# A second filling rate for the end of the RWKV stage in a hybrid recurrent layer

## The chip, the cores and the metric

The kernel runs on one core of a Trainium2 chip. The time is device microseconds (us) of one launch; before the change the median of three runs is 1621.25 us (1619.7 to 1624.62). The change is measured against that. One execution was taken with the hardware profiler; the rows below come from it, with times in us from the start of its span.

## What is computed

One layer of a bidirectional diffusion backbone on 640 tokens (512 latent, 128 context), width 1024, in float32. Three mixers share one projection of the normalised input; gates merge them; a SwiGLU feed-forward follows:

```python
(hq, hf_f, hf_b, hi, hg, rw, mq, mk, mv, mo, mg, gates) = _split(h @ P['w_in'][l], IN_WIDTHS)
y_a, new_a = _hgrn2(hq, hf_f, hf_b, hi, hg, ...)      # gated linear recurrence, 4 heads
y_b, new_b = _rwkv7(rw, grid, ...)                    # RWKV-7: delta-rule scan, 8 heads
y_c, new_c = _mlstm(mq, mk, mv, mo, mg, ...)          # matrix memory, 4 heads
g_a, g_b, g_c = jnp.split(jax.nn.sigmoid(gates.astype(F32)), 3, axis=-1)
merged = g_a * (y_a @ wb[0]) + g_b * (y_b @ wb[1]) + g_c * (y_c @ wb[2])
x = x + g1 * _rms(merged @ P['w_out'][l], nw[1])
u, gt = jnp.split(h @ P['w_ffn_in'][l], 2, axis=-1)
x = x + g2 * _rms((silu(gt) * u) @ P['w_ffn_out'][l], nw[3])
```

The scale, shift and gate vectors `sh1 .. g2` are `silu(cond) @ w_ada` in six pieces; the last four of them are needed only after the merge.

## The kernel before

Activations lie transposed, channels on partitions, tokens along the free dimension in two halves of 320 (`HN`). A float32 product is made of three passes over split operands (`whi`, `wlo` for weights; `h_hi`, `h_lo` for activations). One block of 128 output channels is a **projection**: one 512 KB weight load on the DMA queue of SyncE (SP), two casts `whi` on ScalarE (ACT), two subtractions `wlo` on VectorE (DVE), and 2 halves x 8 blocks x 3 passes = 48 matmuls of 128x320 into two PSUM tiles `pj`. GpSimd (POOL) has no part in it.

The stages follow each other: the input norm with a first part of the conditioning; RWKV; HGRN and mLSTM woven together (called the mixer stage here); merge and output projection; feed-forward.

RWKV goes over four pairs of heads (`p`), and in each pair over three groups of chunks (`gi`). A group has a wide part, `prepare(gi)` (the inverse of a triangular matrix by doubling: products `q`, `y2`, `xp`, `rr`, `dy`), and a chain of dependent steps, `scan(gi)`: per chunk three small products into one tile `z` (from the state `Ss`, from `zs`, from `SV`), with VectorE and ScalarE between any two, and at the end the output products `oc`. `weave` runs `scan(gi - 1)` beside `prepare(gi)`. After the last group nothing of RWKV is left to run beside `scan(2)`; `finish` then normalises the output (`rwkv_post`, head sums `hs`).

Work that nothing in RWKV waits for is used as **filling**. The generator `fill()` holds, in the order of the string `ORDER`, 24 gate projections (`g`), 4 + 4 projections for HGRN and mLSTM output gates (`h`, `o`), each evacuated by ScalarE into a tile `gs` and stored to DRAM (`gates`), and 16 conditioning units (`a`: two 512 KB loads `wada`, 8 row products `acc`, a ScalarE copy `rows`, and two products `col_` that the next unit issues). A projection takes two pulls of the generator, of which the first issues all its work; a conditioning unit takes one. The tail of the order is `gga` repeated, 5 pulls each.

`run_over` decides when a pull is made. It adds `rate[at[0]]` for every step of the main work and pulls one item for every whole unit:

```python
def run_over(main, under, rate):
    a = 0.0
    for _ in main:
        a += rate[at[0]]
        while a >= 1.0:
            a -= 1.0
            next(under, None)
```

`at[0]` is the number of the pair, and `FILL` has one rate for each pair. In the mixer stage the same function runs with `FILL2`, one rate for each mLSTM head; what is left of the filling after that stage is issued by `run(fl)` behind it. The instructions of all this go to a scheduler that places them on the five engines' queues, each in order; the steps of RWKV have a priority ahead of the filling (`OFFD`). So the tables `FILL` and `FILL2` decide near which step of the main work a projection stands, and the scheduler decides between which of its instructions.

In the mixer stage an HGRN head has per level two operand tiles `hT` (made by GpSimd, VectorE and ScalarE) and a product `hg_`; a level ends in `hAT` or `hAD`, and after the last level come the output products `hop`, transposes `hotr`, and the result `ya`. The mLSTM head beside it has products `ms`, `kv`, `kx`, `np_`, `nq`. The first products of the merge are `pj<-ya,whi`.

The mLSTM part begins with its gates: a projection `mg`, evacuated to `G`, then a chain over ScalarE and VectorE (`LF`, the scans `gc` and `mrow`, `PK`). ScalarE's queue holds the evacuation of HGRN's first projection (`hT<-pj`, line 396) and the exponential `PK` (line 1308) in one order; TensorE's transposes `btr` (line 557) wait for the first.

Of the kernel before, what the change touches and what calls it, by code (L numbers as in the profile page):

```python
# [36 lines left out]
SPO = ()  # L37
PADD = (1, 3, 5, 7)
FRONT = 0.25
FILL = (0.145, 0.145, 0.16, 0.155)  # L40
WRES = 10
ADAB = 12
RB2 = 2
# [212 lines left out]
def build(tc, **A):  # L256
# [36 lines left out]
    with ExitStack() as top:  # L293
# [246 lines left out]
        def weave(*streams):  # L540

            live = [[g, r, 0.0] for g, r in streams]
            while live:
                x = min(live, key=lambda a: a[2])
                try:
                    next(x[0])
                    x[2] += 1.0 / x[1]
                    yield
                except StopIteration:
                    live.remove(x)  # L550
# [56 lines left out]
        at = [0]  # L607

        def first(g, offset):

            while True:
                try:
                    if offset:
                        with tc.high_priority(offset):
                            next(g)
                    else:
                        next(g)
                except StopIteration:
                    return
                yield  # L620
# [9 lines that stand above are left out]
# [5 lines left out]
        with ExitStack() as rs:  # L635
# [377 lines left out]
            def front_ahead():  # L1013

                for x in fr:
                    yield
                    while at[0] < 3 and Rs[at[0] + 1].get("ready"):
                        yield

            def chain(*gens):  # L1020
                for g in gens:
                    yield from g

            def finish(p):
                rwkv_post(p, Rs[p]["osum"], Rs[p]["wg"], Rs[p]["yb"])
                yield

            def rwkv():
                last = None
                for p in range(4):  # L1030
                    while not Rs[p].get("ready"):
                        yield next(fr)
                    at[0] = p
                    elem, prepare, scan = rwkv_pair(p, Rs[p])
                    for gi in range(3):
                        g = chain(elem(), prepare(0)) if gi == 0 else prepare(gi)
                        yield from weave((last, SRATE[p]), (g, 1.0)) if last else g
                        last = scan(gi)
                        if gi == 2:
                            last = chain(last, finish(p))  # L1040
                yield from last

            run_over(weave((first(rwkv(), OFFD), 1.0), (first(front_ahead(), OFFF), FRONT)), fl, FILL)

        with ExitStack() as ms, ExitStack() as mr:
# [786 lines left out]
```

## Time and profile before

| | |
|---|---|
| median of 3 runs | 1621.25 us (1619.7 to 1624.62) |
| the profiled execution's own time | 1623.08 us |
| its span, first to last instruction | 1621.3 us |
| mean granted TensorE clock | 0.976 of 2.4 GHz |
| busy TensorE / VectorE / ScalarE / GpSimd | 95% / 70% / 48% / 17% |
| RWKV's last group alone, to the end of its outputs | 562.76 to 589.25 us |
| last mixer head, first `htr` to first merge product | 957.49 to 1003.03 us |

The profiled execution is 1.83 us above the median of the runs, and 1.78 us of its time lie around the span. A matmul's duration in a row includes its pipeline, so matmuls in a row start every 0.147 us and show 0.31 us each; distances between starts are the time they take. A granted clock of 1.00 is 2.4 GHz and 0.50 is 1.2 GHz.

### The profile page before, as it was taken

To read this page: it belongs to the slowest core of one execution; us is meant where nothing else is said; L and a number is where in the kernel's file an instruction comes from. 1 tells how busy PE (TensorE), PEld (TensorE's weight loads), DVE (VectorE), ACT (ScalarE), POOL (GpSimd) and SP (SyncE) were. 2 spreads that over 40 slices of the span, in tenths; PEclk is the share of its full clock that TensorE was granted. 3 is DMA by queue.
4 is the path that set the end of the run, shared out by engine and by line. 5 is a ranking of instruction groups with operands and counts; after the bars stand their busy time and mean duration, and the time that the engine had idled before them with its cause. 6 is when DMAs were issued, how large, how long until landed. Compare 5 with 4: busy or idle time off the path is not lost. (4 is left out here: it accounts for less than half of the span.)

```text
span 1621.3 us, 34724 instructions
## 1 busy us (share of the span) xinstructions
PE 1540.6 (95%) x14194; PEld 1418.1 (87%) x14194; DVE 1131.9 (70%) x2355; ACT 782.8 (48%) x1546; POOL 275.7 (17%) x347
## 2 busy tenths in 40 slices
PE   6999999999999988899999999999999999999996
PEld 2988888888877778889798988999999999999996
DVE  6788788687777644786758578772887386586576
ACT  5364455454454334666476666223553343243244
POOL 2110110110110100211303031000123241341211
PEclk9999999999999969999999999999989999999998
DMA  9222222212122313232332332643512222222322
GB/s 361 71 75 88 74 71 80 95 50 88 66 73 95 113 49 103 70 99 78 94 100 85 100 101 95 201 145 108 155 37 86 95 79 76 82 88 68 99 94 97
DMA packets 63791, 157.35 MB, mean 97 GB/s; under 512 B 7432, under 2 KB 27912, under 8 KB 63504
## 3 DMA queue, kind: packets, MB, share of 16 engines
q1 hardware_dynamic: 63488, 155.13, 29.5%
q8 instruction: 111, 1.82, 0.5%
q14 instruction: 48, 0.39, 0.1%
q10 hardware_dynamic: 144, 0.00, 0.0%
HBM read 136.73 MB, written 18.37 MB: 96 GB/s over the span
## 5 line engine op out<-in xcount | busy, mean ns | idle before, releaser
L277 PE MATMUL pj<-h_hi,whi 128*128 128x320 f32 x1560 | 495.0, 320 | 5.4 <-ACT t L396 2.7
L277 PE MATMUL pj<-h_lo,whi 128*128 128x320 f32 x1560 | 494.4, 317 | 0.0
L277 PE MATMUL pj<-h_hi,wlo 128*128 128x320 f32 x1560 | 493.2, 317 | 0.0
L262 DVE TENSOR_TENSOR wlo<-raw,whi 128x512 fp32r<-128x512 f32 (+1 forms) x318 | 228.5, 726 | 130.7 <-ACT whi L344 106.2
L277 PEld LDWEIGHTS pj<-h_hi,whi 128*128 128x128 f32 x1560 | 296.3, 191 | 12.0 <-ACT t L396 3.7
L277 PEld LDWEIGHTS pj<-h_lo,whi 128*128 128x128 f32 x1560 | 296.7, 190 | 3.2
L277 PEld LDWEIGHTS pj<-h_hi,wlo 128*128 128x128 f32 x1560 | 296.9, 190 | 2.8
L344 ACT CAST whi<-raw 128x512 fp32r<-128x512 f32 (+1 forms) x264 | 156.8, 599 | 219.6 <-PE pj L277 209.4
L277 PE MATMUL pj<-a,whi 128*128 128x320 f32 x704 | 155.3, 309 | 0.0
L277 PEld LDWEIGHTS pj<-a,whi 128*128 128x128 f32 x704 | 117.7, 188 | 0.2
L277 PE MATMUL pj<-a,wlo 128*128 128x320 f32 x352 | 108.8, 309 | 0.0
L277 PE MATMUL pj<-t_hi,whi 128*128 128x320 f32 x288 | 89.1, 309 | 1.1 <-DVE u L262 1.1
L277 PE MATMUL pj<-t_hi,wlo 128*128 128x320 f32 x288 | 89.1, 309 | 0.1
L277 PE MATMUL pj<-t_lo,whi 128*128 128x320 f32 x288 | 89.0, 309 | 0.0
L262 DVE TENSOR_TENSOR wlo<-sm,whi 128x512 fp32r<-128x512 f32 x72 | 68.1, 946 | 11.4 <-ACT whi L1684 8.5
L1684 ACT CAST whi<-sm 128x512 fp32r<-128x512 f32 x72 | 44.4, 621 | 64.4 <-PE pj L277 50.2
L1678 POOL TENSOR_TENSOR sm<-raw 128x512 f32<-128x512 f32 x36 | 49.0, 1360 | 110.3 <-DMA raw<-wff 72.5
L277 PEld LDWEIGHTS pj<-a,wlo 128*128 128x128 f32 x352 | 66.1, 188 | 0.0
L277 PE MATMUL pj<-hl,whi 128*128 128x320 f32 x256 | 56.5, 310 | 0.6 <-ACT hl L1462 0.6
L1684 ACT CAST whi<-raw 128x512 fp32r<-128x512 f32 x54 | 33.5, 620 | 45.6 <-PE pj L277 37.7
L277 PEld LDWEIGHTS pj<-t_hi,whi 128*128 128x128 f32 x288 | 54.1, 188 | 1.3 <-DVE u L262 1.3
L277 PE MATMUL acc<-raw,sc 128*32 128x256 f32 (+1 forms) x320 | 40.7, 437 | 14.8 <-DMA raw<-wada 14.8
(659 smaller groups left out, 2988.0 us busy)
## 6 DMA issues: line engine op xcount, KB each, us to landing
raw<-wmix SPq DMA_DIRECT2D x76, 512.0 KB, 3.5
raw<-wada SPq DMA_DIRECT2D x48, 512.0 KB, 5.6
raw<-wff SPq DMA_DIRECT2D x44, 512.0 KB, 3.7
gates<-gs SPq DMA_DIRECT2D x64, 160.0 KB, 1.8
raw<-wff SPq DMA_DIRECT2D x24, 384.0 KB, 3.2
gs<-gates SPq DMA_DIRECT2D x24, 320.0 KB, 3.1
raw<-wbr SPq DMA_DIRECT2D x12, 512.0 KB, 4.3
raw<-wout SPq DMA_DIRECT2D x8, 512.0 KB, 5.0
```

Of the source, the lines that this page charges most:

```text
L262: dve.tensor_tensor(out, a, b, op)
L277: newest[0] = pe.matmul(out, lhsT=lhsT, rhs=rhs, start=start, stop=stop, skip_group_check=more).ins
L344: act.copy(hi[:, :w], raw[:, o:o + w])
L1678: pool.tensor_tensor(o, x, y, op)
L1684: act.copy(hi, x)
```

## The change

The rate table gets a fifth entry, and when the last group of the last pair begins, `at[0]` is set to 4, which selects it. The rate of that group goes from 0.155 to 0.34; the steps before it keep 0.155. `front_ahead`, which also reads `at[0]`, is exhausted by then. Nothing else differs.

```diff
-FILL = (0.145, 0.145, 0.16, 0.155)
+FILL = (0.145, 0.145, 0.16, 0.155, 0.34)
...
                     for gi in range(3):
+                        if p == 3 and gi == 2:
+
+                            at[0] = 4
                         g = chain(elem(), prepare(0)) if gi == 0 else prepare(gi)
```

From there to the end of RWKV the main work has 28 steps (19 of `prepare(2)`, 5 of `scan(1)`, 4 of `scan(2)` with `finish`). With the remainder carried in, 0.155 makes 5 pulls of them (two projections and a conditioning unit) and 0.34 makes 10 (four and two). Five pulls are exactly one period `gga`, so every later pull finds the same kind of item at the same step as before, one period on. In the mixer stage 21 pulls are made either way. Before, five pulls were left for `run(fl)` after that stage (one projection, one conditioning unit and the last columns among them); now none is left, and the mixer stage's last pull issues the last columns where it issued a projection.

How the queues move, at three places. **TensorE, the last scan of RWKV** (`z`, from the last product `dy` of `prepare(2)` on). Before:

```order
L277 MATMUL z<-Ss,AX_7763 64x64 x2
L277 MATMUL z<-Ss,AX_7792 64x64 x2
L277 MATMUL z<-zs,Yf 64x64 x4
L277 MATMUL z<-SV,BT_7784 64x64 x2
L277 MATMUL z<-SV,BT_7834 64x64 x2
L277 MATMUL z<-Ss,AX_7763 64x64 x2
L277 MATMUL z<-Ss,AX_7792 64x64 x2
L277 MATMUL z<-zs,Yf 64x64 x4
```

Now:

```order
L277 MATMUL z<-Ss,AX_7763 64x64 x2
L277 MATMUL z<-Ss,AX_7792 64x64 x2
L277 MATMUL pj<-h_lo,whi 128x320
L277 MATMUL pj<-h_hi,wlo 128x320
L277 MATMUL pj<-h_hi,whi 128x320
L277 MATMUL pj<-h_lo,whi 128x320
L277 MATMUL z<-zs,Yf 64x64 x4
L277 MATMUL pj<-h_hi,wlo 128x320
L277 MATMUL pj<-h_hi,whi 128x320
L277 MATMUL pj<-h_lo,whi 128x320
L277 MATMUL pj<-h_hi,wlo 128x320
L277 MATMUL pj<-h_hi,whi 128x320
```

Where steps of the scan stood next to each other, runs of 4 to 5 projection matmuls stand between them. The same holds back to the end of `scan(1)`: from the `z<-zs` at 562.76 us to the end of `oc`, 76 of the 96 moved matmuls stand in 16 runs of 3 to 7; two stand just ahead of it, and 18, with the 8 row products of the conditioning unit, between `oc` and the projection `mg`.

**TensorE, the last mixer head** (last levels `hg_`, ahead of the output products `hop`). Before:

```order
L277 MATMUL kv<-vs,mkt 128x129
L277 MATMUL pj<-h_hi,wlo 128x320
L277 MATMUL pj<-h_hi,whi 128x320
L277 MATMUL pj<-h_lo,whi 128x320
L277 MATMUL hg__12926<-hq,hT_12924 32x32 x20
L277 MATMUL pj<-h_hi,wlo 128x320
L277 MATMUL np__13000<-v_8302,mD 128x129
L277 MATMUL kv<-vs,mkt 128x129
L277 MATMUL np__13000<-v_8302,mD 128x129 x2
L277 MATMUL pj<-h_hi,whi 128x320
```

Now:

```order
L277 MATMUL hg__12897<-hT_12887,hT_12886 32x32 x20
L277 MATMUL hg__12930<-hT_12920,hT_12919 32x32 x20
L277 MATMUL kx<-vs,mkt 128x129
L277 MATMUL hg__12970<-hT_12960,hT_12959 32x32 x20
L277 MATMUL hg__13022<-hT_13012,hT_13011 32x32 x20
L277 MATMUL kv<-vs,mkt 128x129
L277 MATMUL hg__13077<-hq,hT_13075 32x32 x20
L277 MATMUL np__13151<-v_8453,mD 128x129 x2
L277 MATMUL kv<-vs,mkt 128x129
L277 MATMUL np__13151<-v_8453,mD 128x129
```

Four levels follow each other with no projection between them; from the first `htr` of this head on, none is left.

**ScalarE, the beginning of the last mixer head** (`hkt` copies the transposes `htr`; `gs` evacuates the projection that stands just ahead of them on TensorE). Before:

```order
L572 ACTIVATE gs<-pj 128x320
L344 CAST whi<-raw 128x512 x2
L1138 COPY hkt<-htr 128x512
L572 ACTIVATE gs<-pj 128x320
L558 COPY mkt<-btr 128x384
```

Now:

```order
L572 ACTIVATE gs<-pj 128x320
L344 CAST whi<-raw 128x512 x2
L1465 CAST hl<-yc 128x640
L572 ACTIVATE gs<-pj 128x320
L1141 COPY hkt<-htr 128x512
L558 COPY mkt<-btr 128x384
```

The second `gs` stands ahead of `hkt` instead of behind it, and a cast `hl` of the merge stage has come in (two more stand a few rows on).

## Rows read from the trace of the kernel before

**Rows 1.** The page: busy time of two engines, and the granted clock in 40 slices.

```profile
PE 1540.6 (95%) x14194; PEld 1418.1 (87%) x14194; DVE 1131.9 (70%) x2355; ACT 782.8 (48%) x1546; POOL 275.7 (17%) x347
...
PEclk9999999999999969999999999999989999999998
```

**Rows 2.** Stretches of the span: length, then busy us (and instructions) of TensorE's matmuls and weight loads, VectorE, ScalarE and GpSimd, the granted clock, the DMA engines' share and GB/s. The first two are RWKV's end, the other four the last mixer head.

```profile
562.76:589.25 26.49, 18.38 (x283) 14.56 (x282) 9.87 (x30) 4.38 (x13) 3.24 (x8) 0.57 0.17 66
589.25:600.85 11.60, 10.91 (x59) 10.29 (x59) 3.25 (x8) 7.10 (x12) 1.43 (x3) 0.81 0.29 87
957.49:968.77 11.28, 9.42 (x89) 7.25 (x86) 6.81 (x17) 5.67 (x13) 4.64 (x6) 1.00 0.56 138
968.77:973.30 4.53, 3.81 (x99) 3.33 (x98) 1.46 (x4) 1.53 (x6) 3.25 (x3) 1.00 0.63 242
973.30:992.86 19.56, 17.68 (x300) 15.94 (x300) 18.82 (x49) 10.05 (x20) 4.52 (x7) 1.00 0.18 52
992.86:1003.03 10.17, 9.17 (x79) 7.81 (x78) 8.15 (x31) 8.15 (x26) 0.00 (x0) 1.00 0.20 68
```

**Rows 3.** Instructions of TensorE in order of time: start us, duration us (of the whole merged row), with the idle time before it and its releaser in brackets. RWKV's last pair while filling stands between its steps.

```profile
549.35 0.42 PE L277 MATMUL z<-Ss,AX 64*64 64x64 f32 x8
549.70 0.41 PE L277 MATMUL pj<-h_hi,whi 128*128 128x320 f32 x1
549.95 0.31 PE L277 MATMUL pj<-h_lo,whi 128*128 128x320 f32 x1
...
550.92 0.45 PE L277 MATMUL z<-zs,Yf 64*64 64x64 f32 x8
...
552.52 0.45 PE L277 MATMUL z<-SV,BT 128*64 128x64 f32 x8
...
560.07 1.05 PE L277 MATMUL acc<-raw,sc 128*32 128x256 f32 x10
```

**Rows 4.** The same view, the end of RWKV after the filling has run out.

```profile
562.76 0.45 PE L277 MATMUL z<-zs,Yf 64*64 64x64 f32 x8
563.88 0.45 PE L277 MATMUL z<-SV,BT 128*64 128x64 f32 x8 [0.68 <-ACT SV L887]
...
580.26 0.67 PE L277 MATMUL z<-Ss,AX 64*64 64x64 f32 x8
581.33 0.69 PE L277 MATMUL z<-zs,Yf 64*64 64x64 f32 x8 [0.39 <-DVE zs L262]
582.75 0.70 PE L277 MATMUL z<-SV,BT 128*64 128x64 f32 x8 [0.73 <-ACT SV L887]
584.20 0.69 PE L277 MATMUL z<-Ss,AX 64*64 64x64 f32 x8 [0.74 <-DVE Ss L268]
...
589.94 0.64 PE L277 MATMUL pj<-h_hi,whi 128*128 128x320 f32 x1 [0.69 <-DVE osum L262]
```

**Rows 5.** The same view: the output products `oc` of a full group at the high and at the low clock.

```profile
541.81 1.15 PE L277 MATMUL oc<-AX,Ss 64*64 64x64 f32 x32
...
573.75 1.97 PE L277 MATMUL oc<-AX,Ss 64*64 64x64 f32 x32
```

**Rows 6.** ScalarE in order of time, the gates of mLSTM (`G` is the second half of the projection `mg`).

```profile
601.84 0.52 ACT L1257 ACTIVATE G<-pj,pcol 128x320 f32<-128x320 f32 x1
...
609.96 1.28 ACT L1308 ACT_TABLE_LOAD   x1 [3.01 <-DVE mrow L1280]
611.25 0.73 ACT L1308 ACTIVATE PK<-mrow 4x640 f32<-4x640 f32 x1
611.89 0.41 ACT L396 ACTIVATE hT<-pj 128x320 f32<-128x320 f32 x1
```

**Rows 7.** TensorE at the same place.

```profile
607.88 0.31 PE L277 MATMUL pj<-h_hi,wlo 128*128 128x320 f32 x1
612.36 0.69 PE L557 MATMUL btr<-cst,hT 128*128 128x128 f32 x2 [4.16 <-ACT hT L396]
...
614.18 0.84 PE L557 MATMUL btr<-cst,hT 128*128 128x128 f32 x3
```

**Rows 8.** ScalarE and the DMA queue of SyncE at the start of the last mixer head.

```profile
958.12 0.59 ACT L1138 COPY hkt<-htr 128x512 f32<-128x512 f32 x1
961.37 0.44 ACT L572 ACTIVATE gs<-pj 128x320 f32<-128x320 f32 x1 [2.66 <-DMA gates<-gs]
961.70 0.75 ACT L558 COPY mkt<-btr 128x384 f32<-128x384 f32 x2
962.33 0.76 ACT L1193 ACTIVATE hT<-hT 128x640 f32<-128x640 f32 x1
962.96 0.60 ACT L1138 COPY hkt<-htr 128x512 f32<-128x512 f32 x1
...
957.32 0.42 SPq L573 DMA_DIRECT2D gates<-gs  x1
```

**Rows 9.** TensorE at the end of the last mixer head.

```profile
992.86 0.46 PE L277 MATMUL hop<-hv,hAT 128*128 128x128 f32 x2
...
995.61 0.39 PE L277 MATMUL hop<-hv,hAT 128*128 128x128 f32 x2
...
1000.75 0.74 PE L1236 MATMUL hotr<-cst,hT 128*128 128x128 f32 x5
```

**Rows 10.** The stretch of the last mixer head again, the instructions on the tiles `pj` alone (columns as in rows 2, without GpSimd).

```profile
957.49:1003.03 45.54, 18.18 (x98) 14.29 (x96) 0.00 (x0) 2.16 (x5) 1.00 0.32 96
```

## The prediction

> **What bounds the kernel now.** The page first: TensorE is busy 95% of the span and VectorE 70%, and the clock line is full but for four dips [rows 1]. So a change that only moves TensorE's work can gain where TensorE stands idle or at the low clock, and no more than is lost there. One of the dips is the end of RWKV. The table of stretches is read second. From 562.76 us to the end of `oc` (26.49 us) the granted clock is 0.57, TensorE's rows cover 18.38 us, and neither VectorE (9.87) nor ScalarE (4.38) is near full: a chain of latencies bounds this stretch [rows 2]. TensorE in order of time says the same: each `z` waits 0.39 to 0.74 us for VectorE or ScalarE, and nothing stands in between [rows 4]. Twelve us earlier the same steps had runs of projections between them, at the high clock and without a wait [rows 3]. That hole is where the moved work goes. The place that gives it up is the last mixer head. There the clock is 1.00 throughout, and in its longest piece (973.30 to 992.86) VectorE is busy 18.82 of 19.56 us: VectorE sets the pace there, not TensorE [rows 2]. So both places are holes of TensorE, one of them filled before the change and the other after it. The question is what each costs.
>
> **What moves.** Two projections and one conditioning unit go from the end of the mixer stage to the end of RWKV: 96 matmuls, 8 row products and their columns on TensorE, four `whi` and four `gs` on ScalarE, four `wlo` on VectorE, and on SP's queue four loads of 512 KB and four stores. GpSimd's queue gets nothing. SP has room at the new place, where the DMA engines are 17% busy [rows 2]. In between, the pulls find the same kinds of item at the same steps, one period on, so I count that stretch at nothing; its cover is its own chain, which does not change. If the scheduler placed it otherwise, that would cost or give a microsecond or two, which the range holds.
>
> **The end of RWKV.** TensorE's own time first. The 18.38 us of rows are mostly at the low clock; `oc` takes 1.97 us there and 1.15 at the high one [rows 5], so the steps are about 18.38 x 0.58 = 10.7 us at the high clock. A run of seven projection matmuls between two `z` takes 549.70 to 550.92, 1.22 us [rows 3]; at 0.147 us each, that is 1.03 and 0.2 for the two changes of shape. So 76 matmuls in 16 runs are 11.2 + 3.2 = 14.4 us. Together 25.1 us, if the clock stays up as it did in rows 3, against 26.49: **1.4 less**. The two matmuls that come ahead of the stretch give 0.5 back. The runs are sized to the gaps: from `z<-zs` to `z<-SV` the chain needs 0.45 + 0.73 = 1.18 us [rows 3, 4] and now gets about 0.36 + 5 x 0.147 + 0.2 = 1.3. With a slack of 0.1, the `wlo` and `whi` that now stand in VectorE's and ScalarE's queues can make a step late. Rows 3 had such work too and show no stall; at the other end all four `wlo` are bare, at some 0.7 us each. I take 0.75 (0 to 3), near the end that rows 3 show. `oc` ends about 0.15 us earlier.
>
> Then from there to the end of the projection `mg`: 11.60 us before [rows 2], of which 0.69 is a wait [rows 4] and, with a granted clock of 0.81, some 1.85 are lost to the low clock; 9.05 remain. Now 18 matmuls (2.65, and 0.4 for two more changes of shape), the row products (ten took 1.05 us in rows 3; I take 1.3) and columns (0.4) come in, and a ScalarE that held 7.10 us of work gets `gs`, `rows` and two casts between the head sums, for which I take a stall of 0.8 (0 to 2.5). That is 14.6 us: **3.0 more**. `mg` ends 2.85 us later.
>
> Half of that is taken back where the mLSTM gates are late anyway. Before, `G` began 0.99 us behind `mg`'s end because ScalarE was still at RWKV's output; TensorE then ran dry at 608.2 and stood 4.16 us for `hT`, which sat behind `PK` [rows 6, 7]. Now ScalarE is done in time (0.2). In the order now, the first half of `hT` stands ahead of `PK`, and the second behind it and one cast: from `G` on, 9.4 us to `PK` [rows 6], then 0.6, 0.5 and 0.4, 11 in all. The second `btr` so comes at 600.85 + 2.85 + 0.2 + 11 = 614.9, where it came at 614.18 [rows 7]; the wait ahead of it is about 3 us instead of 4. **RWKV's end costs 0.8** (from -1.5, no stalls, to +5, all of them). In short: 16 us of work go in for about a microsecond.
>
> **The last mixer head.** TensorE's projections covered 18.18 us of its 45.54 [rows 10], but TensorE was not what it waited for, so their going shortens little. Three terms:
> - ScalarE's queue. Before, `hkt` at 958.12 stood ahead of the `gs` that waited 2.66 us for a store on SP's queue [rows 8]. Now that `gs` is ahead. Behind its 961.37 come `hkt`, `mkt`, `hT`, a cast `hl` and the second `hkt`, at pitches of 0.33 and 0.63: it begins at 964.15 instead of 962.96, and the first level waits for it. **+1.2** (0, if the store lands earlier, to 2).
> - Steps that stood behind projections in TensorE's queue come earlier: **-0.6**. In the piece where VectorE is 96% busy nothing is to be had; in the other 26 us VectorE is 16.4 busy [rows 2]. Between 0 and -6, nearer 0, because the waits that rows 8 show there are ScalarE's.
> - The clock. Without projections, TensorE's rows cover 40.1 - 18.2 = 22 us of the 45.5 [rows 2, 10], less than the share at which RWKV's end had 0.57. If the clock falls, VectorE hides it up to `hop`. The five groups of `hop` (992.86 to 995.98) and `hotr` (0.74) [rows 9] lie bare: (3.1 + 0.74) x 0.71 = 2.7 us by the ratio of rows 5. Bounds 0 and 2.7; I take **+1.8**, nearer the end that rows 2 show for a stretch without filling.
>
> The Trainium skill speaks against the change here: its page "TensorE: Matmul & The Clock Gate", section "Part 1: The HAM clock gate", says that the low clock is the default and that only activity releases it. By that rule the last term would be the full 2.7, and the total 4.1 us instead of 3.2; that the clock was down in RWKV's end [rows 2] agrees with it, and no run here yet shows the mixer head without filling.
>
> **Sum.** 0.8 + 1.2 - 0.6 + 1.8 = 3.2 us. On the profiled execution that is 1623.08 + 3.2 = 1626.3; that execution lay 1.83 us above the median of the runs, so for the median **1624.5 us**, 0.2% more. A difference of 0.3% (4.9 us) is about what a measurement of this kernel can tell from no change.
>
> **Rivals.**
> - **Two holes of the same depth** (the forecast): work moves from one hidden place to another. 1620 to 1626. Chance 0.50.
> - **The chain at the mixer's end is laid bare, slower.** The price is the low clock over the whole head: `hop` and `hotr` in full (2.7), the seven level products and the `nq`, `np` steps 0.3 us each where VectorE waits for them (some 2.5), `hkt` 1.2, and at RWKV's end 2 for stalls: 8 us, **1629**. For it: the clock of 0.57 in rows 2. Against it: VectorE's 96%, which leaves it waiting for little. It decides when the granted clock of the four mixer pieces is about a half and VectorE's share in the long one falls under 90%. Chance 0.28.
> - **The mixer head was bound by filling, faster.** Every product of that head stood behind 5 to 15 projection matmuls in an in-order queue. If that, and not VectorE, delayed its first and last pieces, up to 6 us of their 26 go, and RWKV's end gives the 1.5 of its lower bound: some 7 us less, **1614**. For it: TensorE covers 83 to 90% of these pieces while VectorE covers 32 to 80% [rows 2]. Against it: the longest waits there are not TensorE's [rows 8]. Chance 0.20.
> - **The rate moves nothing**, because the scheduler puts the projections back. The order shows them between the steps, so 0.02: 1621.
>
> **How the numbers follow.** The forecast and the last rival are within 0.3% (0.52), the second is slower (0.28), the third faster (0.20). The range reaches from the faster rival to the slower one, each with about a microsecond for what it doesn't settle, and leaves the ends of both outside: 1615 to 1630. The forecast's own range is 1620 to 1626.
>
> **What would show it.** After the change, the stretch from `z<-zs` to the end of `oc` should be 25 to 27 us long with a granted clock above 0.95 and projections between the steps; the second `btr` should come within 2 us of 614.2, after a wait of about 3 us; the head from the first `htr` to the first merge product should be 46 to 49 us long (45.54 before) with a granted clock well under 1.00, and VectorE still above 90% in its long piece. I am wrong if that head gets more than 3 us shorter, if the clock there stays at 1.00, or if RWKV's end takes more than 5 us longer.

## The result: slower by 0.6%, and the profile after

| | before | after |
|---|---|---|
| median of 5 runs each, us | 1621.25 (1619.35 to 1624.62) | 1630.64 (1626.07 to 1631.17) |
| ratio, 95% interval | | 1.0058 (1.0042 to 1.0074) |
| the profiled execution: span, us | 1621.3 | 1629.4 |
| its mean granted clock | 0.976 | 0.975 |

The forecast was 1624.5 us, no change that can be measured; its range ended at 1630. The time came out 0.64 us above it, where the rival "laid bare" had put it (1629).

The two profiled executions are compared by landmarks of TensorE's timeline:

| from, to | before | after | difference |
|---|---|---|---|
| start to the first `oc` of RWKV | 175.05 | 177.93 | +2.88 |
| to the group of `oc` that begins at 540.73 (543.46 after); its second half opens [rows 5] | 365.68 | 365.53 | -0.15 |
| to the first `htr` of the mixer stage | 127.55 | 129.38 | **+1.83** |
| to the first `htr` of the last head | 289.21 | 289.16 | -0.05 |
| to the first merge product `pj<-ya` | 45.54 | 50.90 | **+5.36** |
| to the first product of the output projection | 87.68 | 89.07 | **+1.39** |
| to the last `rr` of the output norm | 517.45 | 514.26 | -3.19 |

The three rows in bold hold what the change touches: 8.58 us. The first row and the last are the same work in the same order, and they differ by execution: over the profiles of this study the first took 175.05 to 179.07 us, the last 514.26 to 519.20. A median of several runs still carries some of that (the medians of the unchanged kernel beside this result and the runs below lie between 1620.07 and 1621.25), so the cause is looked for stretch by stretch. The last row as the windows of three kernels have it (before, after, and a later one; columns as in rows 2): equal instruction counts, unequal lengths.

```profile
1090.71:1608.16 517.45, 509.74 (x3459) 506.73 (x3457) 333.35 (x565) 224.89 (x455) 118.42 (x89) 0.98 0.28 87
```

```profile
1101.97:1616.23 514.26, 505.41 (x3459) 502.74 (x3457) 334.49 (x565) 225.01 (x455) 118.18 (x89) 0.99 0.28 88
```

```profile
1072.52:1591.72 519.20, 511.33 (x3459) 508.37 (x3457) 333.48 (x565) 225.09 (x455) 118.43 (x89) 0.98 0.27 87
```

**RWKV's end, after.** Windows of the changed kernel: the tail from `z<-zs` to the end of `oc`, then from the second `btr` to the products `csp` behind it.

```profile
566.66:591.09 24.43, 24.43 (x360) 20.38 (x359) 10.74 (x31) 6.21 (x17) 2.79 (x7) 1.00 0.27 93
617.40:626.99 9.59, 9.24 (x48) 8.73 (x49) 6.75 (x10) 6.79 (x13) 0.00 (x0) 0.74 0.16 57
```

The tail is 2.06 us shorter than in [rows 2], the granted clock 1.00 where it was 0.57, and TensorE busy throughout, with 77 instructions more in it. TensorE at the second `btr` (for [rows 7]), with the last matmul of the low clock (starts 0.27 us apart before it, 0.15 behind it):

```profile
617.40 0.90 PE L557 MATMUL btr<-cst,hT 128*128 128x128 f32 x3 [3.77 <-ACT hT L396]
617.96 0.62 PE L277 MATMUL pj<-h_hi,wlo 128*128 128x320 f32 x1
618.37 0.47 PE L277 MATMUL pj<-h_hi,whi 128*128 128x320 f32 x1
...
622.11 0.46 PE L277 MATMUL pj<-h_hi,wlo 128*128 128x320 f32 x1
622.37 0.34 PE L277 MATMUL pj<-h_hi,whi 128*128 128x320 f32 x1
```

From the `oc` of the table it comes after 73.94 us, where it came after 73.45: 0.5 later. In [rows 7] the wait ended at the first `btr`; now it ends at the second, so the whole low-clock time lies behind that one.

**The last mixer head, after.** ScalarE and the DMA queue of SyncE at its start (for [rows 8]; the first `htr` is at 962.00), then four windows from the first `htr` to the first merge product (for [rows 2]), and the instructions on `pj` there (for [rows 10]).

```profile
962.63 0.72 ACT L1465 CAST hl<-yc 128x640 fp32r<-128x640 f32 x1
965.72 0.44 ACT L572 ACTIVATE gs<-pj 128x320 f32<-128x320 f32 x1 [2.37 <-DMA gates<-gs]
966.05 0.58 ACT L1141 COPY hkt<-htr 128x512 f32<-128x512 f32 x1
...
969.30 0.59 ACT L1141 COPY hkt<-htr 128x512 f32<-128x512 f32 x1 [0.77 <-PE htr L1139]
```

```profile
961.81 0.42 SPq L573 DMA_DIRECT2D gates<-gs  x1
```

```profile
962.00:972.00 10.00, 7.36 (x51) 6.33 (x48) 5.18 (x11) 5.56 (x12) 3.61 (x4) 0.83 0.46 138
972.00:982.00 10.00, 7.82 (x104) 6.05 (x107) 6.20 (x15) 4.45 (x10) 5.42 (x5) 0.77 0.08 21
982.00:1002.29 20.29, 12.47 (x268) 10.28 (x263) 18.66 (x52) 7.00 (x12) 4.96 (x6) 0.50 0.10 25
1002.29:1012.90 10.61, 6.73 (x41) 5.74 (x40) 7.09 (x26) 6.36 (x27) 0.00 (x0) 0.82 0.21 65
...
962.00:1012.90 50.90, 0.16 (x3) 0.01 (x1) 0.00 (x0) 0.44 (x1) 0.68 0.19 55
```

The first `hkt` starts 4.05 us after the first `htr` (0.63 before), the second 7.30 (5.47 before). From 15.4 us after the first `htr` on the clock is at its low level (0.50), up to 2.4 us behind the first `hop`; VectorE is still 92% busy in the long piece.

TensorE at the end of the head and in the merge (for [rows 9]):

```profile
1001.27 1.23 PE L277 MATMUL nq<-Cs,mq 128*128 128x129 f32 x4 [0.57 <-ACT nd L1397]
1002.29 0.64 PE L277 MATMUL hop<-hv,hAT 128*128 128x128 f32 x2
...
1010.98 1.34 PE L1239 MATMUL hotr<-cst,hT 128*128 128x128 f32 x5 [2.78 <-DVE hT L1229]
1012.90 0.90 PE L277 MATMUL pj<-ya,whi 128*128 128x320 f32 x2 [0.58 <-DVE hk L268]
...
1020.91 0.85 PE L277 MATMUL pj<-hl,whi 128*128 128x320 f32 x4 [1.19 <-ACT hl L1465]
```

### The profile page after: what moved, and what is told of

Same layout as the page of the kernel before. It is cut to its first block, busy times and chain, and to the rows that moved or that the text cites. A ratio compares the mean times of both kernels' runs of the same rounds, so it can differ in the third digit from the quotient of the medians.

```text
span 1629.4 us, 34729 instructions
## 1 busy us (share of the span) xinstructions
PE 1542.9 (95%) x14194; PEld 1418.8 (87%) x14194; DVE 1133.7 (70%) x2355; ACT 781.1 (48%) x1544; POOL 276.0 (17%) x347
## 5 line engine op out<-in xcount | busy, mean ns | idle before, releaser
L1681 POOL TENSOR_TENSOR sm<-raw 128x512 f32<-128x512 f32 x36 | 48.5, 1347 | 111.3 <-DMA raw<-wff 75.3
L277 PEld LDWEIGHTS pj<-t_hi,wlo 128*128 128x128 f32 x288 | 54.8, 190 | 2.8 <-DVE wlo L262 2.8
L1687 ACT CAST whi<-raw 128x512 fp32r<-128x512 f32 x54 | 33.5, 620 | 45.6 <-PE pj L277 37.6
```

The lines of the kernel that those rows point to most:

```text
L277: newest[0] = pe.matmul(out, lhsT=lhsT, rhs=rhs, start=start, stop=stop, skip_group_check=more).ins
L1681: pool.tensor_tensor(o, x, y, op)
L1687: act.copy(hi, x)
```

## The experiments

Two questions. What makes the emptied head 5.4 us longer: the low clock, or ScalarE's queue, where `hkt` now stands behind a `gs` that waits for a store? And where should the 16 us of filling have come from? Times are medians, ratios are to the kernel before, run in turns on the same chip (1621.17 us beside runs 1, 2 and 5; 1620.07 beside 3, 4, 6 and 8; 1620.15 beside 7, 9 and the repeat of 6). "Pulls" are counts by pair and head as in the part on the change; places of matmuls are from the order of the queues.

**1. No store to wait for.** The last projection is evacuated into the last head's part of `yc`, which is written only at that head's end.

```diff
-                    gs = gt_p.tile([128, HN], F32, name="gs")
+                    gs = half(spare[0], n) if name == "g2_7" else gt_p.tile(...)
...
+            spare[0] = yc[:, 3]
```

> The changed kernel, but the last gate projection is evacuated into a part of yc that is still free, not into the two gs buffers, so its evacuation, which stands ahead of hkt on ScalarE, has no store to wait for. Queue theory (of the 5.4 us that the last head grew, about 3.3 come from hkt standing behind a gs that waits 2.4 us for a store, and some 2 from the low clock): the first hkt starts 1.0 to 1.5 us after the first htr (4.05 in the changed kernel), the head from first htr to first merge product takes 47.5 to 48.5 us (50.90), the time falls by 2.5 to 3.5 us against the changed kernel, to about 1627.5. Clock theory (the head is long because TensorE runs it at 1.2 GHz, and the wait is hidden behind that): the head stays above 50 us and the time within 1 us of 1630.6.

Measured: 1628.87 us, ratio 1.0044 (1.0031 to 1.0057). ScalarE at the start of its last head (first `htr` at 960.00):

```profile
960.63 0.43 ACT L573 ACTIVATE yc<-pj 128x320 f32<-128x320 f32 x1
960.96 0.58 ACT L1143 COPY hkt<-htr 128x512 f32<-128x512 f32 x1
963.82 0.58 ACT L1143 COPY hkt<-htr 128x512 f32<-128x512 f32 x1
```

The first `hkt` comes after 0.96 us (1.0 to 1.5 expected), the second after 3.82; the head takes 47.50 us, 3.40 less. By the stretch that is the lower end of what the queue theory expected, and the clock theory, which had it above 50, is out as the only cause. The median fell by 1.8, where 2.5 to 3.5 were expected.

**2. Something for TensorE to do, and nothing else.**

```diff
                     level(T1, T2, hh)
+                    dummy(hd)
...
+                def dummy(hd):
+                    if hd == 3:
+                        acc = pj_p[0].tile([128, HN], F32, name="pj")
+                        for i in range(12):
+                            mm(acc, ya[:, 0, 0, 0:128], h[0][:, i % 8, 0:HN], i == 0, i == 11)
```

> The changed kernel with 12 products of 128x320 behind each of the eight levels of the last HGRN head, whose results nobody reads: 96 products as before the change, but without loads, casts, evacuations and stores. Clock theory: the granted clock of the head goes back to 1.00, the head to 45.5 to 46.5 us, the merge starts at the high clock, the time is near 1624. Queue theory: hkt still starts about 4 us after the first htr, so only the clock's part comes back: the head takes 48 to 49.5 us, the merge another 1 us less, the time 1627 to 1629. If TensorE's own work were the bound in the head, it would get longer than 51 us.

Measured: 1631.81 us, ratio 1.0065 (1.0052 to 1.0078): not faster than the change. Its head is 49.00 us, as the queue theory had it, and the stretch behind it 0.7 shorter; by the stretches it should be some 2 us faster, and the queue theory's 1627 to 1629 was missed. Its profile has 518.29 us behind the output projection's start, 4.03 more than the changed kernel's, which the edit doesn't touch; whether that is all of the difference in the medians stays open. `hkt` still comes 4.37 us after the first `htr`. From the first `htr` to `hop` the granted clock is 0.96:

```profile
962.94:1002.12 39.18, 33.63 (x498) 29.93 (x495) 31.22 (x73) 16.42 (x32) 13.05 (x15) 0.96 0.17 54
```

**3. Both repairs at once.** The edits of 1 and 2 together.

> The changed kernel with both repairs of its last head at once: the last projection evacuated into yc (no store to wait for ahead of hkt), and the 96 products that nobody reads. Queue theory (hkt's wait 3.3 us, the clock about 2, nothing else): the head from first htr to first merge product takes 45 to 46.5 us, as before the change (45.54), and ya to hl 6.5 us again; hop comes 35 to 36 us after the first htr. If something else is missing from the sum, the head stays above 47.

Measured: 1623.52 us, ratio 1.0014 (1.0003 to 1.0024). The head takes 42.76 us: 2.8 **less** than before the change, which nobody expected. The windows from the first `htr` to `hop` and from there to the merge, of run 1 (emptied, `hkt` on time) and of run 3 (the same with the unread products):

```profile
960.00:996.79 36.79, 23.52 (x409) 19.12 (x407) 29.61 (x75) 16.90 (x33) 13.73 (x15) 0.76 0.19 57
996.79:1007.50 10.71, 6.83 (x40) 5.84 (x39) 7.84 (x27) 6.35 (x27) 0.00 (x0) 0.82 0.19 64
```

```profile
962.47:996.20 33.73, 30.44 (x492) 27.18 (x489) 29.67 (x72) 16.62 (x32) 12.70 (x15) 1.00 0.22 63
996.20:1005.23 9.03, 7.04 (x56) 6.17 (x54) 5.22 (x20) 4.53 (x17) 0.00 (x0) 0.99 0.21 73
```

VectorE and ScalarE do the same work up to `hop` (29.61 and 29.67, 16.90 and 16.62 us); TensorE does 83 matmuls **more** and is done 3.1 us sooner, at a granted clock of 1.00 and not 0.76. So with `hkt` on time the low clock costs the emptied head 4.74 us (47.50 against 42.76), and the late `hkt` another 3.40 on top (50.90 against 47.50). In the other order it divides otherwise: the products alone gave 1.90 back (run 2), and the early `hkt` behind them 6.24 (49.00 against 42.76). The two overlap; free of the order is only their sum, 8.14. Against it stands the 2.78 by which the head with the real filling was longer (45.54). Run 3 has neither the projections' loads, casts, evacuations and stores nor an `hkt` as late as before (4.45 us, 5.47 before); which of these makes the 2.78 was not tested.

**4. Emptying the last head without filling RWKV's end.** The kernel before, with more pulls in the mixer stage.

```diff
-FILL2 = (0.13, 0.14, 0.11, 0.16)
+FILL2 = (0.16, 0.165, 0.14, 0.20)
```

> The kernel before the change with higher mixer rates (0.16, 0.165, 0.14, 0.20): 26 pulls in the mixer stage and none left over, so the last head is emptied, but the work goes into the earlier heads and not to RWKV's end. No gs stands just ahead of hkt here. Theory: RWKV's end as before; the earlier heads are 11 to 16 us longer (first to last htr 300 to 305, where it was 289), for want of a hole there; the last head, with the clock's part alone, 47 to 48.5 us; 1634 to 1640. Rival (heads are chains of fixed length): 1622 to 1626.

Measured: 1634.85 us, ratio 1.0087 (1.0072 to 1.0102). The time is as expected, the places only in part: 7 us of the work went ahead of the first `htr` (88.09 us from RWKV's last output products, 81.14 before), and the stage from the first to the last `htr` took 292.2, not 300. The last head, emptied down to 48 matmuls, took 46.0. That is less than the 47 to 48.5 expected; its second `hkt` came after 3.22 us, and from there to `hotr` it took 41.0 (37.8 before). Where TensorE is dense the work costs its full time: 48 projection matmuls more ahead of the first `htr` are those 7 us, and 45 more behind the second head's chain 8.8 (59.06 us for 50.25). The chains themselves move both ways (the first head's 54.02 us become 41.01, the second's 42.54 become 48.50), so heads are not chains of fixed length.

**5. The same tail, another donor.** The changed kernel, with five pulls fewer in the mixer stage, so that five are left for the last head as before. First spread over the heads, then out of the first two:

```diff
-FILL2 = (0.13, 0.14, 0.11, 0.16)
+FILL2 = (0.10, 0.11, 0.085, 0.12)
```

```diff
-FILL2 = (0.13, 0.14, 0.11, 0.16)
+FILL2 = (0.07, 0.08, 0.11, 0.16)
```

The pulls of the four heads are 4, 5, 3, 4 in the first (called a), 3, 3, 4, 6 in the second (called c), and 6, 5, 4, 6 before the change.

> The changed kernel with the mixer stage's rates lowered (0.10, 0.11, 0.085, 0.12 for 0.13, 0.14, 0.11, 0.16), so that 16 pulls are made there instead of 21 and five are left over behind it, as before the change. The end of RWKV and the last head are both filled; the earlier heads give up the 16 us of work. Theory of the wrong donor (RWKV's end costs about 2 us; the change lost because it took the work from the one head that has nothing else to fill it): the last head is back at 45 to 47 us; earlier heads, whose holes the next head's own projections can fill, get shorter together by 5 to 16 us, and the time is 1608 to 1618, faster than before the change. Rival (the heads are chains of fixed length whatever fills them): the time is that before the change plus RWKV's 1.8, 1622 to 1625.

> As the run before, but the five pulls are taken from the first two heads alone (rates 0.07, 0.08, 0.11, 0.16). Theory of the wrong donor: last head 45 to 47 us, 1608 to 1618, with the gain between the first htr of the stage and that of the third head. Rival (chains of fixed length): 1622 to 1625, with the first two heads as long as before and at a lower clock.

Measured: a 1617.40 us, ratio 0.9979 (0.9970 to 0.9988); c 1610.89, ratio 0.9940 (0.9927 to 0.9954). Both times are as the donor theory expected, and the last heads take 46.52 and 44.92 us (45.54 before). The first head's chain (`htr` to `hotr`) and the dense stretch behind it, before and in c:

```profile
668.28:722.30 54.02, 47.27 (x591) 42.35 (x589) 42.59 (x109) 27.43 (x65) 12.69 (x15) 0.94 0.30 89
722.30:772.75 50.45, 50.45 (x348) 50.23 (x349) 32.71 (x55) 36.89 (x65) 5.09 (x5) 1.00 0.24 81
```

```profile
669.45:710.62 41.17, 37.09 (x532) 33.81 (x530) 35.66 (x97) 22.66 (x53) 13.12 (x15) 1.00 0.27 78
710.62:752.71 42.09, 42.09 (x291) 41.91 (x292) 24.29 (x40) 31.76 (x59) 5.80 (x5) 1.00 0.25 78
752.71:800.14 47.43, 39.83 (x544) 35.27 (x542) 40.15 (x102) 24.89 (x56) 12.92 (x15) 0.93 0.29 85
```

The dense stretch is TensorE from end to end in both kernels: 57 matmuls fewer are 8.36 us, 0.147 each. That is about half of what c saves: from the first `htr` of the stage to that of the third head it takes 181.25 us for 197.26, 16.0 less. The other part is the first head's chain, 12.9 shorter, in which TensorE is not busy throughout (47.27 of 54.02 us); what shortened it is looked for in run 7. The third row of c shows where 4.9 of the saving went back: the second head's chain, 42.54 us before, takes 47.43.

**6. What the tail itself is worth.** Rates of c, but the kernel before, so RWKV's end is unfilled and ten pulls are left over. The profile is that of a repeat of the same kernel.

> The kernel before the change with the mixer rates of the run that took five pulls from the first two heads (0.07, 0.08, 0.11, 0.16): the end of RWKV stays unfilled, ten pulls are left over behind the mixer stage, of which the last head can cover five. Theory (the end of RWKV is a hole that holds 16 us of work for about 2): the first htr comes 2 us earlier than with the filled tail, the mixer stage is as long, and some 93 projection matmuls stand bare between hotr and the merge, 13 to 15 us: 1610.9 - 2 + 14, so 1620 to 1625. Rival (the gain of that run came from the mixer rates alone): 1607 to 1612.

> The kernel of the run without the filled tail once more, for its profile: 1623 to 1628. By the theory some 94 projection matmuls stand between the last hotr and the first merge product, which takes 14 to 17 us instead of 2.3, and the first htr comes 2 us earlier after RWKV's last full outputs than with the filled tail. By the rival that stretch is under 6 us.

Measured: 1626.65 us, ratio 1.0038 (1.0025 to 1.0051), 1.7 above what was expected; the repeat 1625.08, as expected. In its profile, the stretch from the last `hotr` to the first merge product (2.29 us in c), and the instructions on `pj` in it:

```profile
988.54:1006.59 18.05, 17.20 (x131) 16.24 (x128) 8.77 (x23) 11.78 (x28) 0.00 (x0) 1.00 0.71 227
...
988.54:1006.59 18.05, 14.97 (x97) 13.92 (x95) 0.00 (x0) 1.75 (x4) 1.00 0.71 227
```

The work that has no hole stands bare: 15.8 us. The filled tail costs 2.6 from the `oc` of the table to the first `htr` (129.73 in c, 127.13 here). So, with the mixer rates of c, filling RWKV's end is worth 13 us in the profiles and 15.8 in the medians.

**7. Half the dose.** The changed kernel with `FILL[4]` 0.25: two pulls more in the tail instead of five, mixer rates as before.

> The changed kernel with 0.25 instead of 0.34 in the last group: two more pulls there than before the change (one projection, 48 matmuls) instead of five, three left over behind the mixer stage. In the order this projection comes out of the first head's chain (105 projection matmuls instead of 152), and the last head keeps its 96. Theory of the donor (filling RWKV's end pays where the work comes from a stretch that TensorE bounds): the first head, 54.0 us from htr to hotr, takes 45 to 47, the last head stays at 45 to 47, RWKV's end costs 0 to 2: 1613 to 1617, faster than before although the tail gets less. Rival (what counts is how full the tail is; the loss is in the last head only): within 2 us of 1621.

Measured: 1638.82 us, ratio 1.0106 (1.0092 to 1.0121): the slowest of all, and against both theories. The matmuls stand where the order had them, and RWKV's end cost nothing (oc to `htr` 127.03). But the four heads took 49.75, 49.49, 47.95 and 46.04 us from `htr` to `hotr`, where they had 54.02, 42.54, 41.50 and 43.26. Two pulls are not a whole period `gga`, so behind them every pull finds another kind of item at its step, and what stands ahead of `hkt` in ScalarE's queue is another. ScalarE at the start of the third head (first `htr` at 871.41):

```profile
870.76 0.42 ACT L396 ACTIVATE mk<-pj 128x320 f32<-128x320 f32 x1
874.25 1.54 ACT L1197 ACTIVATE hT<-hT 128x640 f32<-128x640 f32 x2 [3.07 <-DVE hT L262]
...
877.05 0.58 ACT L1141 COPY hkt<-htr 128x512 f32<-128x512 f32 x1
...
881.03 0.59 ACT L1141 COPY hkt<-htr 128x512 f32<-128x512 f32 x1 [1.87 <-PE htr L1139]
```

`hkt` waits behind exponentials that wait for VectorE, and TensorE stands with it. That gives a third theory, which the heads of all profiles were then held against: **a head's length is set by when its second `hkt` starts.** Start of that copy after the head's first `htr`, and the length to `hotr` (us):

| head | second `hkt` | length | difference |
|---|---|---|---|
| before, heads 1 to 4 | 16.26, 5.43, 3.94, 5.47 | 54.02, 42.54, 41.50, 43.26 | 37.8, 37.1, 37.6, 37.8 |
| c, heads 1 to 4 | 3.65, 10.35, 6.57, 5.40 | 41.17, 47.43, 44.89, 42.63 | 37.5, 37.1, 38.3, 37.2 |
| 0.25, heads 1 to 4 | 11.43, 7.66, 9.62, 7.65 | 49.75, 49.49, 47.95, 46.04 | 38.3, 41.8, 38.3, 38.4 |
| after, head 4 (emptied) | 7.30 | 48.98 | **41.7** |
| run 1, head 4 (emptied) | 3.82 | 45.59 | **41.8** |
| run 3, head 4 (unread products) | 4.45 | 40.94 | 36.5 |

A filled head is the start of that copy and some 37 to 38.5 us; an emptied one 41.7. One stands out, the second head of this run, where a product waited 3.15 us for `nd`. The filled heads of the other runs, run 8 left out, lie between 36.5 and 38.9; the last head of run 4, with half its filling, has 41.0, and that of run 2, with unread products and a late `hkt`, 39.2. So it was not the number of projections in the first head's chain (152 before, 113 in c, 105 here, for 54.0, 41.2 and 49.8 us) that set its length. This theory was made from these heads; the second part of run 9 is its test.

**8. The first chain step by priority.** Run c with `htr`, `hkt` and `hpr` under the priority that RWKV's steps have.

```diff
+                    with tc.high_priority(PRI):
+                        tr = ps2.tile([128, 4, 128], F32, name="htr", tag="H")
...
```

> The run that took five pulls from the first two heads, with a priority for the beginning of each HGRN head: htr, hkt and hpr are placed as early as their operands allow, ahead of projections, gs and mLSTM's copies. Queue theory carried on (a head's length depends on how soon hkt gets through ScalarE's queue): the second and third heads, 47.4 and 44.9 us from htr to hotr at a clock of 0.93 to 0.96, lose what they have over 41.2; their TensorE keeps the high clock: 1600 to 1607. Rival (the beginning is not what sets a head's end; VectorE is): within 2 us of 1610.9.

Measured: 1634.84 us, ratio 1.0090 (1.0076 to 1.0103), 24 us behind c; neither theory had a loss. TensorE in the last head:

```profile
946.49 0.66 PE L1141 MATMUL htr<-cst,hT 128*128 128x128 f32 x4 [1.41 <-DVE hT L263]
...
957.12 0.63 PE L1141 MATMUL htr<-cst,hT 128*128 128x128 f32 x4 [2.11 <-DVE hT L263]
...
972.20 0.80 PE L278 MATMUL hg__12591<-hT,hT 128*64 128x64 f32 x20
```

The first head's `htr` does come 16 us earlier (653.02, 669.45 in c). But TensorE now waits for its operands and for those of the second `htr`, here 10.6 us later, and behind the `hpr` of the second stand 76 projection matmuls ahead of the first level, which comes 25.7 us after the first `htr` (7.39 before). The second `hkt` no longer tells the length: the head takes 60.93 us, 49.6 behind that copy. Here a priority for the chain's first links let the filling in between them and the rest.

**9. Two more donors.** The tail of the change, pulls 1, 5, 4, 6 and pulls 2, 4, 4, 6.

```diff
-FILL2 = (0.13, 0.14, 0.11, 0.16)
+FILL2 = (0.03, 0.13, 0.11, 0.16)
```

```diff
-FILL2 = (0.13, 0.14, 0.11, 0.16)
+FILL2 = (0.05, 0.11, 0.11, 0.16)
```

> As the run that took five pulls from the first two heads, but all five from the first head and the stretch ahead of it (rates 0.03, 0.13, 0.11, 0.16). In the order the 96 matmuls come out of the stretch from RWKV to the first htr (402 instead of 450) and out of the first head's chain (110 instead of 152). Theory of the donor: that stretch is 7 us shorter, the first head 42 to 47 us, the others 41 to 45 and the last head 45 to 46.5: 1607 to 1613. Rival (chains of fixed length): 1618 or more.

> As that run, with rates 0.05, 0.11, 0.11, 0.16: two pulls in the first head, four in the second. The projections stand as in the run with 0.07 and 0.08 (113 and 271 matmuls in the first head's chain and behind it), only the conditioning units and with them hkt's place in ScalarE's queue differ: no gs stands ahead of hkt in the first three heads. Theory: the second and third heads, 47.4 and 44.9 us there, take 42 to 45, and the time is 1605 to 1610. Rival (hkt's place in the queue is of no account where the head is filled): 1609 to 1613.

Measured: the first 1616.28 us, ratio 0.9967 (0.9954 to 0.9980), outside what was expected (its eleven runs spread from 1609.48 to 1618.43); the second **1607.25**, ratio 0.9915 (0.9902 to 0.9928), the fastest of all. In the first the stretch ahead of the first `htr` is 6.9 us shorter than with the unmoved rates (122.47 for 129.38), as expected, but its first head has its second `hkt` after 10.52 us and takes 48.02. In the second TensorE has, up to the end of the third head, the same instructions in each chain and each dense stretch as in c; what differs is what stands ahead of `hkt`. In c's second head those were two exponentials that waited 2.56 us for VectorE, in its third a `gs` that waited for a store (its row comes first; first `htr` at 850.70). Then ScalarE in the second head of the last run (first `htr` at 754.81), and its first two chains with the dense stretch between them:

```profile
855.67 0.44 ACT L572 ACTIVATE gs<-pj 128x320 f32<-128x320 f32 x1 [3.75 <-DMA gates<-gs]
```

```profile
756.62 0.60 ACT L1141 COPY hkt<-htr 128x512 f32<-128x512 f32 x1
...
759.60 0.59 ACT L1141 COPY hkt<-htr 128x512 f32<-128x512 f32 x1
```

```profile
671.73:712.70 40.97, 37.08 (x532) 33.79 (x530) 35.20 (x97) 22.40 (x57) 12.93 (x15) 1.00 0.27 78
712.70:754.81 42.11, 42.11 (x292) 41.83 (x292) 29.03 (x50) 33.44 (x57) 5.87 (x5) 1.00 0.24 82
754.81:798.15 43.34, 40.20 (x544) 35.41 (x542) 34.30 (x92) 23.04 (x54) 14.11 (x15) 0.96 0.31 93
```

The second head's `hkt` starts after 4.79 us instead of 10.35, and the head takes 43.34 instead of 47.43, the third 41.51 instead of 44.89; 42 to 45 were expected, so the third is 0.5 below. The differences to the second `hkt` are 38.55 and 37.57. In the second head the comparison is not clean: ten VectorE steps for the head's operands and three exponentials also moved ahead of its first `htr` (VectorE 34.30 us in the chain instead of 40.15), and a lighter VectorE could have shortened it as well. In the third nothing of that moved; the chain in c and in this run:

```profile
850.70:895.59 44.89, 39.58 (x543) 34.98 (x541) 35.12 (x97) 22.62 (x57) 12.51 (x15) 0.96 0.30 96
...
848.70:890.21 41.51, 38.59 (x543) 33.75 (x541) 35.18 (x97) 22.91 (x57) 13.29 (x15) 1.00 0.36 99
```

VectorE and ScalarE have the same work there, the second `hkt` starts 2.63 us earlier (3.94 for 6.57), and the chain is 3.38 shorter. From the first to the last `htr` it is 268.9 us, where before had 289.2.

## Why the prediction was wrong

By its own sum of 3.2 us, against the 8.58 of the touched stretches:

- **RWKV's end, 0.8 forecast, +1.83 measured.** What was worked out was right in the main: the tail at the high clock and without a stall (25 to 27 us forecast, 24.43), the second `btr` within 2 us, its wait still 3.77. The sum ended there, though, and 1.34 us more come behind it: the low clock that follows the wait now lies behind the second `btr`, 16 matmuls of it instead of 10, some 0.7 us, and `mtr` waits 0.35 for ScalarE; the rest was not traced.
- **ScalarE's queue, +1.2 forecast, +1.83 measured** for the second `hkt` (7.30 against 5.47 after the first `htr`). The mechanism was right, and the net is inside the bounds (0 to 2), but partly by luck: without the wait for the store the emptied head starts its second `hkt` at 3.82 (run 1), so the wait costs 3.48 there, and 1.65 of it is hidden by steps that come earlier. The first `hkt` was not priced, and the second waits for it through TensorE, where the second `htr` stands behind the `hpr` that needs it.
- **Earlier steps and the clock, -0.6 and +1.8 forecast, together +3.89 measured** (41.68 against 37.79 from the second `hkt` to `hotr`). This is the step that failed. I took the clock's price from `hop` and `hotr` alone, 2.7 at most, since VectorE hides it up to `hop`. From the second `hkt` the fourth level comes 1.8 us later and the eighth 1.5, so the VectorE-bound middle did hide it; but the first levels are not VectorE's (6.20 busy of 10 us), nor is the way from the last level to `hop`, another 1.6, with its `np` and `nq` in turn with ScalarE; `hop` to `hotr` adds 0.8. Unread products, which bring the clock back, take 2.5 of the 3.89 away where `hkt` is late (39.15 in run 2), and 5.3 where it is on time (41.77 in run 1, 36.49 in run 3). My test for it, VectorE under 90% in the long piece, was wrong too: it stayed at 92%, and the loss was at both ends of that piece. Nor did my list of what would prove me wrong hold a head longer than 49 us.
- **The merge, nothing forecast, +1.39 measured**, at a low clock and with 1.19 of wait for `hl` (0.55 before). From `hotr` to the merge 0.36 was gained. 1.83 + 1.83 + 3.89 - 0.36 + 1.39 = 8.58.

The rival **laid bare** had the sign, the place and almost the time, the last in part by luck: it counted 2 us of stalls in RWKV's end that did not come and nothing for the merge, and its own sign, VectorE under 90%, did not show. It was likelier than the 0.28 I gave it, because the granted clock of 0.57 in [rows 2] was a measurement of just such a stretch. By the rule of the Trainium skill's page "TensorE: Matmul & The Clock Gate", section "Part 1: The HAM clock gate", only activity releases the low clock; runs 1 and 3 agree: work that nobody reads brought the clock from 0.76 to 1.00, and the head became shorter. My forecast bent its price down. The rival **filling-bound** fell as a whole, and its premise was misread: the trace before has no projection matmul between 957.49 and 967.72 us, the first ten of the head. It has a grain of truth: without the real filling, but with unread products and `hkt` on time, the head was 2.78 us shorter. (The clock line of [rows 1] has three dips, not four; nothing hangs on it.)

What I did not ask is which stretch should give the work up. I compared two holes. The mixer stage also has 150 us in which TensorE is busy without a gap (50.45 us at a stretch, clock 1.00). Taking the work from the first two heads and the stretch between them, with the tail that the change fills, is worth 10.3 to 12.9 us (1610.89 against 1621.17, 1607.25 against 1620.15). Only 8.4 of that is the dense stretch; the first head's chain became 13 us shorter, with its second `hkt` that much sooner, which I did not foresee either. The first part of run 9 took 6.9 us out of a dense stretch too, but there the first head's second `hkt` stood late (10.52 us), and it ended at 1616.28.

## What to carry to other kernels

Filling put into a hole pays its full time where it comes out of a stretch in which TensorE is never idle; taken out of another hole it can leave a chain at the low clock, and the price is paid in all links that another engine doesn't hide, not only in the last ones. A table of rates moves more than amounts: an uneven number of pulls, or pulls moved between heads, shifts which item stands next to which step, and here heads changed by up to 13 us with that; so look in each in-order queue at what stands ahead of the chain's first copies. Where two causes meet in one stretch, repair each alone and both together: the price of one depends on the other. Compare such variants by stretches between landmarks, since stretches that no edit touches differed by up to 4.9 us.

## What the runs showed of the hardware

- Eighty-three matmuls more in a 34-us stretch made it 3.1 us shorter, with equal work on VectorE and ScalarE (runs 1 and 3): the granted clock was 0.76 without them and 1.00 with them.
- Stretches of equal instructions in equal order differ between executions of one program: 175.05 to 179.07 us in the first, 514.26 to 519.20 in the last. In the changed kernel's first stretch the clock was 0.93 from 12 to 60 us, before the change 1.00.
